# Output projection, second half: for each token tile the products with the first two head pairs first, for both column halves

## The chip, the cores and the metric

The kernel runs on one core of one Trainium2 chip. The metric is the device time of one execution, in microseconds (us). It is one launch that computes one transformer-like block on 512 tokens.

## The reference, cut to what matters

```python
z = h @ w_in                                    # h: adaLN-modulated RMSNorm of x, [512, 1024]
rec = _hgrn2(...)                               # 4 heads of 128: mix columns 0..511
att = _dsa_attention(...)                       # 8 heads of 64: mix columns 512..1023
mix = concatenate([rec, att]) @ w_out           # [512, 1024] @ [1024, 1024]
x = x + g1 * mix
h2 = _rms(x, norm2_g) * (1 + sc2) + sh2
x = x + g2 * _hier_moe(h2, ...)                 # router (4 + 16 logits), top group, top 2 of 4 experts;
                                                # 16 experts: (silu(h2 @ w1) * (h2 @ w3)) @ w2
```

All of it is float32. The vectors g1, sc2, sh2, g2 come from `silu(c) @ w_ada`, whose last parts are still being computed while attention ends.

## The kernel before, in words

**Precision by splitting.** A float32 product is made of three faster ones. A weight piece of 128 x 1024 (`raw`) is cast to `wh` on ACT, and DVE subtracts to get the rest `wl`. The activations are split the same way, into two halves of a tile `mix`. One call of `mm3` is three products of 128x512: mix-high by wh, mix-high by wl, mix-low by wh. `split_gen` does this for the pieces of w_in and then for the eight pieces of w_out, NZ to NZ+7, each after DVE has multiplied it by `g1b` (so that the projection comes out gated). Piece NZ + 4*half + 2*c + p holds the rows of two k-tiles (`mix` 4*half+2p and the next) and the columns of half c.

**Who sets the order.** Each step of the program is a Python generator. A small list scheduler, `Desk`, runs at build time: it takes the generator whose next step could start first by its own estimates (ties by a table of ranks), and so writes one fixed instruction order for each engine. Every engine then runs its list strictly in order and waits by semaphores. All instructions are recorded by one helper line, L177, so the program's tile names say what a row is. DMAs that carry their own line numbers (L1290, L1291) are issued by ACT from its own list.

**The output projection.** `out_gen` has two halves. Half 0 multiplies mix 0 to 3 (the recurrence's heads). Half 1 multiplies mix 4 to 7 (four pairs of attention heads, attention unit j gives mix 4+j) and runs while the last attention unit, attention 3, ends. Half 1 goes over four token tiles t and in each over the two column halves c. For one (t, c) a PSUM bank of the tag `z` (there are two such banks) collects 12 products: six with mix 4 and 5 (p = 0, piece NZ+4+2c) and six with mix 6 and 7 (p = 1, piece NZ+5+2c). `add_gen` then adds the bank to the residual `xm[t]` on DVE, and that frees the bank.

**What follows a tile.** `post_gen(t)` is started when tile t reaches c = 1. For each column half (kh) it transposes xm on PE (`a<-cs,xm`, four of 128x128, a PSUM tile `a`), copies the result to `hT` on ACT, and multiplies by the router's weights on PE (`u<-wr,hT` for even tiles, `o<-wr,hT` for odd ones, four for each kh). `norm_gen` squares and sums on ACT (`sc`). Then DVE makes the logits `L` and the second pass of `h2` (`h<-h,ss,sh2b`), `store_gen` lets ACT issue two DMAs (h2 and xm to memory, 512 KB each), and the routing follows on DVE. `first_gen` gathers the first expert's tokens when all tiles are through (`z<-oh,h`), and the MoE products (`h<-wh,xh`, ...) come after these.

**The end of attention 3.** PE makes `u<-PT,vv` (16 products, the attention's output), and then a chain follows whose parts are on different engines: `sq` on ACT, a mean by products on PE (`a<-sq,csm`), Ln and Exp on ACT, a multiplication on DVE, `mix` on ACT and DVE. Beside it, the last steps of adaLN run: `acc<-dd,cT,acc` on DVE, `a<-acc,ones` on PE, which lead to sh2b and gs2b and their transposes (`a<-cs,sh2b`, `a<-cs,gs2b`). One of the pieces, NZ+5, gets its place in a pool `mw` that can only be opened when attention 0 to 3 are done.

Of the kernel before, what the change touches and what calls it, by code (L numbers as in the profile page):

```python
# [9 lines left out]
F32 = mybir.dt.float32  # L10
F32R = mybir.dt.float32r
BF16 = mybir.dt.bfloat16
# [3 lines left out]
OP = mybir.AluOpType  # L16
# [4 lines left out]
T, D, P = 512, 1024, 128  # L21
# [3 lines left out]
MARK = -3e38  # L25
# [8 lines left out]
TMP2 = {"nl": 2, "oh": 3, "sq": 2, "zs": 2}  # L34
# [35 lines left out]
class Desk:  # L70
# [26 lines left out]
    def spawn(self, gen, name, rank):  # L97
        self.count += 1
        self.tasks.append(Task(gen, name, RANK[rank], self.at, self.last, self.count))

    def mark(self, name):
        self.done[name] = self.at
# [110 lines left out]
def hymba_kernel(ctx, tc, x, xT, w_ada1, w_ada, w_in, w_out, w_r, w1, w3, w2, vec, n2g, rb, rel, cst, t5, out):  # L213
    nc = tc.nc
    desk = Desk()
    spawn, mark, run = desk.spawn, desk.mark, desk.run
    sp = nc.sync
    act, dve, pool, pe = (desk.engine(e, n) for e, n in (
        (nc.scalar, "act"), (nc.vector, "dve"), (nc.gpsimd, "pool"), (nc.tensor, "pe")))
# [13 lines left out]
    def place4(tag, shape, dtype, name):  # L233
        return ar.tile(shape, dtype, tag=tag, name=name)
# [6 lines left out]
    def bank(shape=None, tag="a"):  # L241
        return ps.tile(shape or [P, 512], F32, tag=tag, name=tag, bufs=BANKS[tag])


    def slot_bank(shape=None, tag="a"):
        yield tag, BANKS[tag]
        return bank(shape, tag), desk.take(tag)
# [11 lines left out]
    def either(size):  # L259
        e = yield {"dve": size * EITHER_D, "pool": size * EITHER_P}  # L260
        return pool if e == "pool" else dve
# [16 lines left out]
    def C(n):  # L278
        a, b = CST[n]
        if b <= CST_W:  # L280
            return cs[:, a:b]
        off = CST["bo64"][0]
        return csm[:, a - off:b - off]
# [19 lines left out]
    area = [None]  # L303

    def tmp(tag, name, shape=None, dtype=F32):
        own, bufs = area[0]
        return own.tile(shape or [P, T], dtype, tag=tag, name=name, bufs=bufs[tag])
# [5 lines left out]
    pair = [None] * KT  # L313
# [21 lines left out]
    NZ = len(order)  # L335
    stream = [w_in[i] for i in order] + [w_out[i] for i in range(8)]
    raws, halves = {}, {}

    def fetch(n):
        if n < len(stream):  # L340
            raws[n] = ring()
            sp.dma_start(raws[n], stream[n])
            desk.done["raw", n] = desk.move()

    def split_gen():
        for n in range(len(stream)):

            need = ["mw"] if n == NZ + 5 else [("used", n - (WPB if HEAD + WPB <= n < NZ + 5 else HEAD if n < NZ else 4))]
            yield [("raw", n)] + (need if HEAD <= n < NZ else ["ada0"] * (n >= NZ))
            raw = raws.pop(n)  # L350
            if n >= NZ:
                eng = yield from either(1.0)
                rv = raw.rearrange("p (k c) -> p k c", k=2)
                c = (n - NZ) // 2 % 2
                eng.tensor_tensor(rv, rv, g1b[:, None, c * 512:c * 512 + 512].to_broadcast([P, 2, 512]), op=OP.mult)
                yield need
            yield "act"
            if WPB <= n < HEAD:
                wh, wl = (place4(f"B{2 * (n - WPB) + i}", [P, D], F32R, "wB") for i in range(2))
            else:  # L360
                own, bufs = (mw, WX) if n == NZ + 5 else (wp, WPB)
                wh = own.tile([P, D], F32R, tag="wh", name="wh", bufs=bufs)
                wl = own.tile([P, D], F32R, tag="wl", name="wl", bufs=bufs)
            act.copy(wh, raw)
            eng = yield from either(1.0)
            eng.tensor_tensor(wl, raw, wh.bitcast(F32), op=OP.subtract)
            halves[n] = wh, wl
            mark(("split", n))
            fetch(n + RING)
# [108 lines left out]
    def mm3(o, ah, al, bh, bl, start, stop):  # L478
        pe.matmul(o, ah, bh, start=start, stop=False)
        pe.matmul(o, ah, bl, start=False, stop=False)  # L480
        pe.matmul(o, al, bh, start=False, stop=stop)
# [33 lines left out]
    spawn(chunk_gen(), "chunks", "split")  # L515
    spawn(norm1_gen(), "norm1", "norm")
    spawn(split_gen(), "splits", "split")
    spawn(line_gen(), "line", "pz")
    for n in range(HEAD):
# [7 lines left out]
    gp = mixer.enter_context(ExitStack())  # L527
# [458 lines left out]
    def mod_rows(dst, r):  # L986
        pool.dma_start(dst, bass.AP(tensor=modD.tensor, offset=modD.offset + r * 512, ap=[[0, P], [1, D]]))
        return desk.move()
# [160 lines left out]
    def gate_gen():  # L1149
        yield ["ada1"]  # L1150
        desk.at += 2500
        desk.at = mod_rows(g2b, 6)

    h2s, routed, px = [None] * 4, {}, []

    def out_gen():
        nonlocal mw, sel, oh0, pair2
        for half in range(2):
            if half:
                yield [("att", j) for j in range(4)]  # L1160
                gp.close()
                mw = ctx.enter_context(tc.tile_pool(name="mw", bufs=1, reuse_waits="tile"))
                mark("mw")
                area[0] = mw, TMP2
                for n, w, v in (("g1", 8, -MARK), ("gm", 8, None), ("em", 16, None), ("e8", 8, None),
                                ("e2", 8, -MARK), ("er", 16, None)):
                    routed[n] = mw.tile([P, 4, w], F32, name=n)
                    if v:
                        pool.memset(routed[n], v)
                sel = mw.tile([P, 4, 16], BF16, name="sel")  # L1170
                oh0 = tmp("sq", "oh0", [P, 4, P])
                pair2 = mw.tile([P, 4, 16, 5], BF16, name="pair")
                pool.tensor_copy(pair2[:, :, :, 0], C("tok")[:, 0:1, None].to_broadcast([P, 4, 16]))
                pool.tensor_tensor(pair2[:, :, :, 1], C("tokT")[:, :, None].to_broadcast([P, 4, 16]),
                                   C("tok")[:, 0:1, None].to_broadcast([P, 4, 16]), op=OP.subtract)
            for a, b in ((a, b) for a in range(4) for b in range(2)):
                c, t = (b, a) if half else (a // 2, a % 2 * 2 + b)
                tt = slice(t * P, (t + 1) * P)
                n = NZ + half * 4 + c * 2
                if half and c:  # L1180
                    spawn(post_gen(t), ("post", t), "post")
                o, mz = yield from slot_bank(tag="z")
                for p in range(2):
                    yield [("split", n + p)]
                    wh, wl = halves[n + p]
                    for k in range(2):
                        kt = 4 * half + 2 * p + k
                        yield [("mix", kt)]
                        mx = pair[kt]
                        kc = slice(k * 512, k * 512 + 512)  # L1190
                        yield "pe"
                        mm3(o, mx[:, 0, tt], mx[:, 1, tt], wh[:, kc], wl[:, kc], p + k == 0, p + k == 2)
                    if t == 3:
                        mark(("used", n + p))
                spawn(add_gen(half, c, t, o, mz), ("add", half, c, t), "use")

    def add_gen(half, c, t, o, mz):
        cc = slice(c * 512, (c + 1) * 512)
        yield [("x", t)] + [("add", 0, c, t)] * half
        yield "dve"  # L1200
        dve.tensor_tensor(xm[t][:, cc], xm[t][:, cc], o, op=OP.add)
        mark(mz)

    sel = oh0 = pair2 = None

    def post_gen(t):
        yield [("add", 1, 0, t)] + [("post", t - 2)] * (t > 1)
# [85 lines left out]
    def first_gen():  # L1293
        yield ["out", ("store", 0), ("sel", 0), ("turned", 3)] + [("add", 1, 1, t) for t in range(4)]
        for _ in range(2):
            t, _m = yield from slot_bank([P, 4, P], "z")
            px.append(t)
            yield "pe"
            pe.matmul(px[-1], onesb, trib[:, 0:1, None].to_broadcast([P, 4, P]), start=True, stop=False)
        for t in range(4):  # L1300
            yield [("store", t), ("sel", t)] + [("pr", 3)] * (t > 0)
            for k in range(KT):
                yield "pe"
                pe.matmul(px[k // 4][:, k % 4], h2s[t][:, k * P:(k + 1) * P], oh0[:, t],
                          start=False, stop=t == 3 and k % 4 == 3)

    spawn(rows_gen(), "rows", "rows")
    spawn(gate_gen(), "gate", "rows")
    spawn(out_gen(), "out", "out")
    spawn(first_gen(), "first", "first")  # L1310

    def split2(n):
# [85 lines left out]
    gate, w = (mw.tile([P, 4, n], F32, name=m) for n, m in ((2, "gate"), (1, "wn")))  # L1398
# [303 lines left out]
```

## Time and profile before

| what | us |
|---|---|
| three runs | 728.30, 727.78, 728.07 (median 728.07) |
| the profiled execution | 727.48 |
| its span in the trace | 725.6 |
| PE busy in the span | 683.1 |
| DVE busy | 630.9 |
| ACT busy | 439.0 |

The span is the time from the first to the last instruction of the trace; the profiled execution's own time is 1.9 us more. "Busy" leaves out the instructions that only issue or branch. A row of the timeline gives the start, the duration, the engine, the line, the operation with its tiles (out <- in) and the count of equal instructions in a row; a bracket gives the idle time of the engine ahead of it and what ended it. Products are pipelined, so the duration of one (0.4 us) is longer than the distance from one to the next (0.23 us).

### The profile page before, as it was taken

How to read it: one execution, taken by the hardware profiler on the slowest of the kernel's cores; microseconds unless marked ns; L12 is line 12 of the kernel's file. 1: busy time of each engine (PE TensorE's matmuls, PEld its weight loads, DVE VectorE, ACT ScalarE, POOL GpSimd, SP SyncE). 2: the span in 40 equal slices, each digit the busy share in tenths (PEclk: the TensorE clock that was granted, in tenths of full speed). 3: DMA queues.
4: the chain of work that ended last, by engine and by line, in shares of the span. 5: the costliest groups of instructions: out<-in, count | busy, mean ns of one | idle time of the engine just before them, and what ended most of it. 6: DMA issues, size and time to landing. Idle time of an engine off the chain costs nothing.

```text
span 725.6 us, 10941 instructions
## 1 busy us (share of the span) xinstructions
PE 683.1 (94%) x3794; PEld 530.9 (73%) x3794; DVE 630.9 (87%) x1057; ACT 439.0 (61%) x670; POOL 202.4 (28%) x104
## 2 busy tenths in 40 slices
PE   3999999999999999999889979999999999999993
PEld 1666778877778776667568858888888888888872
DVE  4637889999999987978866889999999999999991
ACT  4326664545557466553343458888777777777770
POOL 0120010001321321122200030165655655556412
PEclk9999999999999999999989999999999999999997
DMA  9947532231120324685697889999999999999502
GB/s 363 406 154 224 190 111 88 89 115 59 56 90 30 117 88 164 225 308 181 188 362 305 315 318 406 390 376 347 365 363 367 354 350 358 364 361 349 187 11 33
DMA packets 57388, 172.84 MB, mean 238 GB/s; under 512 B 11954, under 2 KB 12530, under 8 KB 56304
## 3 DMA queue, kind: packets, MB, share of 16 engines
q1 hardware_dynamic: 45168, 150.54, 56.1%
q0 software_dynamic: 10720, 17.24, 8.5%
q10 hardware_dynamic: 1440, 4.31, 1.5%
q8 instruction: 32, 0.52, 0.3%
q14 instruction: 28, 0.23, 0.1%
HBM read 167.50 MB, written 15.24 MB: 252 GB/s over the span
## 4 chain that ended last, share of the span: by engine, by line
PE 50%; DMA 21%; DVE 14%; issue 10%; ACT 3%; SPq 0%; POOL 0%; POOLq 0%; DVEq 0%; ACTq 0%
PE z L177 30%; PE a L177 14%; DMA w<-in_w_dram 13%; DVE wl L177 8%; DMA out_dram<-yo,idx 6%; PE u L177 2%; PE h L177 2%; PE o L177 2%; DMA dd<-in_w_ada_dram 1%; DMA chunk<-in_w_ada_dram 1%; DVE yo L177 1%; DVE xl L177 1%; DVE oh L177 1%; ACT wh L177 1%; ACT sq L177 1%
## 5 line engine op out<-in xcount | busy, mean ns | idle before, releaser
L177 ACT CAST wh<-w 128x1024 fp32r<-128x1024 f32 x168 | 174.5, 1054 | 44.2 <-PE h L177 30.9
L177 DVE TENSOR_TENSOR wl<-w,wh 128x1024 fp32r<-128x1024 f32 x168 | 196.6, 1216 | 2.4 <-ACT wh L177 2.0
L177 PE MATMUL z<-hx,wh 128*128 128x512 f32 x496 | 163.1, 409 | 1.1 <-DVE hx L177 0.6
L1358 POOL DMA_INDIRECT out_dram<-yo,idx x16 | 123.7, 7730 | 120.8 <-DVE wl L177 64.1
L177 PEld LDWEIGHTS z<-hx,wh 128*128 128x128 f32 x496 | 88.8, 189 | 27.1 <-issue 8.7
L177 PE MATMUL h<-wl,xh 128*128 128x512 f32 x256 | 101.4, 396 | 0.0
L177 PE MATMUL h<-wh,xh 128*128 128x512 f32 x256 | 100.8, 394 | 0.0
L177 PE MATMUL h<-wh,xl 128*128 128x512 f32 x256 | 100.6, 393 | 0.0
L177 ACT CAST wh<-raw 128x1024 fp32r<-128x1024 f32 x64 | 67.1, 1052 | 55.3 <-PE z L177 48.0
L177 PE MATMUL z<-hx,wl 128*128 128x512 f32 x248 | 97.6, 394 | 0.0
L177 DVE TENSOR_TENSOR wl<-raw,wh 128x1024 fp32r<-128x1024 f32 x64 | 81.6, 1286 | 6.8 <-ACT wh L177 6.5
L177 PEld LDWEIGHTS h<-wl,xh 128*128 128x128 f32 x256 | 48.5, 189 | 12.9 <-DVE wl L177 3.0
L177 PEld LDWEIGHTS h<-wh,xh 128*128 128x128 f32 x256 | 48.5, 189 | 10.2
L177 PEld LDWEIGHTS h<-wh,xl 128*128 128x128 f32 x256 | 48.4, 189 | 10.1 <-DVE xl L177 0.3
L177 PE MATMUL y<-wh,hh 128*128 128x512 f32 x128 | 53.0, 414 | 2.0 <-DVE yo L177 2.0
L177 PEld LDWEIGHTS z<-hx,wl 128*128 128x128 f32 x248 | 46.8, 189 | 10.3
L177 PE MATMUL y<-wl,hh 128*128 128x512 f32 x128 | 50.6, 396 | 0.0
L177 PE MATMUL y<-wh,hl 128*128 128x512 f32 x128 | 50.6, 395 | 0.0
L177 PE MATMUL z<-wh,mix 128*128 128x512 f32 x128 | 48.3, 421 | 0.0
L177 DVE SCALAR_TENSOR_TENSOR acc<-dd,cT,acc 128x512 f32<-128x512 f32 x56 | 43.8, 782 | 3.6 <-DMA dd<-in_w_ada_dram 3.0
L177 POOL TENSOR_TENSOR dd<-b 128x512 f32<-128x512 f32 (+1 forms) x14 | 17.2, 1242 | 93.5 <-PE a L177 79.0
L1353 POOL DMA_INDIRECT xe<-h2D,idx x15 | 17.1, 1140 | 80.5 <-DVE idx L177 46.3
(290 smaller groups left out, 1145.2 us busy)
## 6 DMA issues: line engine op xcount, KB each, us to landing
w<-in_w_dram SPq DMA_DIRECT2D x164, 512.0 KB
raw<-in_w_in_dram SPq DMA_DIRECT2D x33, 512.0 KB
dd<-in_w_ada_dram SPq DMA_DIRECT2D x64, 256.0 KB
raw<-in_w_dram SPq DMA_DIRECT2D x24, 512.0 KB
chunk<-in_w_ada_dram SPq DMA_DIRECT2D x8, 1024.0 KB
raw<-in_w_out_dram SPq DMA_DIRECT2D x8, 512.0 KB
lineR<-lineD POOLq DMA_DIRECT2D x4, 640.0 KB, 17.6
xt<-in_xT_dram SPq DMA_DIRECT2D x4, 512.0 KB
```

The source lines that it names most:

```text
L177: r = f(*a, **k)
L1353: pool.indirect_dma_start(out=dst, out_offset=None, in_=h2D, in_offset=bass.IndirectOffsetOnAxis(ap=ix, axis=0), bounds_check=T - 1, oob_i ...
L1358: pool.indirect_dma_start(out=out, out_offset=bass.IndirectOffsetOnAxis(ap=ix, axis=0), in_=y, in_offset=None, bounds_check=T - 1, oob_is_ ...
```

## The change

The second half of `out_gen` now opens both z banks of a tile at once, and goes through (p, c) in the order p0 c0, p0 c1, p1 c0, p1 c1 instead of c0 p0, c0 p1, c1 p0, c1 p1. `post_gen(t)` is started when the loop reaches p1 c0. The pool `mw` is opened by a task of its own, `places_gen`, so that `out_gen` no longer waits there for attention 0 to 3. The pieces of w_out are split in the order NZ+4, NZ+6, NZ+5, NZ+7. The number of products is the same.

```diff
     def split_gen():
-        for n in range(len(stream)):
+        for n in [*range(NZ + 5), NZ + 6, NZ + 5, NZ + 7]:
...
+    def places_gen():
+        nonlocal mw, sel, oh0, pair2
+        yield [("att", j) for j in range(4)]
+        gp.close()
+        mw = ctx.enter_context(tc.tile_pool(name="mw", bufs=1, reuse_waits="tile"))
+        mark("mw")
...
+        for t in range(4):
+            banks = []
+            for p in range(2):
+                for c in range(2):
+                    if p == 0:
+                        banks.append((yield from slot_bank(tag="z")))
+                    elif c == 0:
+                        spawn(post_gen(t), ("post", t), "post")
+                    o, mz = banks[c]
+                    yield from piece_mm(o, 1, c, p, t)
+                    if p:
+                        spawn(add_gen(1, c, t, o, mz), ("add", 1, c, t), "use")
...
+    spawn(places_gen(), "places", "load")
```

`piece_mm` holds the six products of one piece, unchanged. The places where the order of an engine's list changes, by the two programs' lists:

On PE, just ahead of the last `u<-PT,vv` products of attention 3 (the rows with a + are the first z products of half 1, tile 0, with mix 4 and 5):

```order
 L177 MATMUL a<-cs,nl 128x128 x4
+L177 MATMUL z<-wh,mix 128x512
+L177 MATMUL z<-wl,mix 128x512
+L177 MATMUL z<-wh,mix 128x512 x2
+L177 MATMUL z<-wl,mix 128x512
+L177 MATMUL z<-wh,mix 128x512 x2
+L177 MATMUL z<-wl,mix 128x512
+L177 MATMUL z<-wh,mix 128x512 x2
+L177 MATMUL z<-wl,mix 128x512
+L177 MATMUL z<-wh,mix 128x512
 L177 MATMUL u<-PT,vv 64x128 x8
```

So 12 products, tile 0's p0 for both column halves, now stand ahead of the 16 u products (eight in each of two PSUM tiles); before, they stood behind the `a<-acc,ones` products.

On ACT, at the end of tile 0 (h_3613 and h_3624 are tile 0's h2 in the two programs; the `hT` copy and the `sc` behind the DMAs are tile 1's, kh = 0):

```order
 L177 ACTIVATE ss_3086<-hsq 128x1
 L177 ACTIVATE ss_3086<-ss_3086 128x1
-L1290 DMA h2D<-h_3613 128x1024
-L1291 DMA out_dram<-xm 128x1024
-L177 ACTIVATE sc,hsq<-xm 128x512
+L177 ACTIVATE sc,hsq<-xm 128x512
+L1305 DMA h2D<-h_3624 128x1024
+L1306 DMA out_dram<-xm 128x1024
 L177 COPY hT<-a 128x512
```

The two DMAs stand ahead of tile 1's first `hT` copy in both programs. On PE, between tile 0's last `u<-wr,hT` and tile 1's first `o<-wr,hT` stood 18 z products and four transposes; now there stand six z products and four transposes.

On PE and ACT, at tile 2 to tile 3. First PE before, the end of tile 3's c0 (z_3877 is the bank of c1, a_3889 the transposes, o_3888 the router's products):

```order
L177 MATMUL z_3877<-wh_3603,mix_2775 128x512
L177 MATMUL a_3889<-cs_75,xm_3074 128x128 x4
L177 MATMUL z_3877<-wh_3646,mix_3210 128x512
L177 MATMUL z_3877<-wl_3647,mix_3210 128x512
L177 MATMUL z_3877<-wh_3646,mix_3210 128x512
L177 MATMUL z_3877<-wh_3646,mix_3528 128x512
L177 MATMUL z_3877<-wl_3647,mix_3528 128x512
L177 MATMUL z_3877<-wh_3646,mix_3528 128x512
L177 MATMUL o_3888<-wr_3083,hT_3887 128x20 x4
```

Then PE in the changed program (a_3899 and o_3898 are the same steps):

```order
L177 MATMUL z_3848<-wh_3614,mix_3547 128x512
L177 MATMUL z_3848<-wl_3615,mix_3547 128x512
L177 MATMUL z_3848<-wh_3614,mix_3547 128x512
L177 MATMUL a_3899<-cs_75,xm_3074 128x128 x4
L177 MATMUL o_3898<-wr_3083,hT_3897 128x20 x4
```

And ACT in the changed program, the stores of tile 2 and what stands behind:

```order
L1305 DMA h2D_92<-h2_3817 128x1024
L1306 DMA out_0_dram<-xm_3073 128x1024
L177 CAST wh_3888<-w_3653 128x1024
L177 ACTIVATE sc_3900,hsq_3088<-xm_3074 128x512
L177 COPY hT_3897<-a_3899 128x512
```

The six z products that stood between the transposes and the router's products are now ahead of both, 12 z products stand between tile 2's last `u<-wr,hT` and a_3899, and ACT's list has a cast of a MoE weight between the stores and `hT`.

## Rows read from the trace of the kernel before

**Rows 1.** The page's first line.

```profile
span 725.6 us, 10941 instructions
```

**Rows 2.** Stretches: busy us of PE, PEld, DVE, ACT, POOL (instructions); granted clock; DMA share; GB/s.

```profile
365.00:368.30 3.30, 3.30 (x22) 2.44 (x23) 3.19 (x3) 0.27 (x1) 0.59 (x1) 0.50 1.00 392
368.30:378.60 10.30, 9.07 (x58) 7.45 (x56) 4.73 (x8) 5.28 (x9) 0.57 (x1) 1.00 1.02 402
378.60:404.20 25.60, 25.56 (x150) 21.44 (x149) 17.66 (x51) 10.51 (x26) 0.00 (x0) 1.00 0.72 274
440.00:690.00 250.00, 250.00 (x1220) 203.35 (x1219) 249.59 (x289) 198.97 (x222) 131.00 (x26) 1.00 0.96 351
```

**Rows 3.** PE in order, attention 3's last head pair and the pause: start, duration, [idle <-releaser].

```profile
355.21 0.43 PE L177 MATMUL u<-PT,vv 128*64 128x128 f32 x2
...
355.99 1.09 PE L177 MATMUL u<-PT,vv 128*64 128x128 f32 x14 [0.34 <-ACT PT L177]
...
364.94 0.68 PE L177 MATMUL a<-acc,ones 128*32 128x128 f32 x8 [4.99 <-DVE acc L177]
...
365.97 0.80 PE L177 MATMUL z<-wh,mix 128*128 128x512 f32 x1
...
368.54 0.60 PE L177 MATMUL a<-cs,sh2b 128*128 128x128 f32 x4
```

**Rows 4.** DVE around the copy of PT.

```profile
353.90 0.68 DVE L177 COPY PT<-a 128x512 f32<-128x512 f32 x1
354.51 0.68 DVE L177 TENSOR_TENSOR xm<-xm,z 128x512 f32<-128x512 f32 x1
```

**Rows 5.** DVE, products of pieces of w_out with g1: ns min/median/max.

```profile
L177 DVE TENSOR_TENSOR raw<-raw,g1b x7: 1211/1216/1718, 300.2 to 373.3; 128x1024 f32<-128x1024 f32 x7
```

**Rows 6.** ACT, the square root's input of attention 3.

```profile
357.11 0.60 ACT L177 ACTIVATE sq<-u 128x512 f32<-128x512 f32 x1 [1.18 <-PE u L177]
```

**Rows 7.** PE in order, tile 0's second column half before the change.

```profile
372.17 0.48 PE L177 MATMUL z<-wh,mix 128*128 128x512 f32 x1
...
373.20 0.50 PE L177 MATMUL z<-wl,mix 128*128 128x512 f32 x1 [0.56 <-DVE wl L177]
...
373.78 0.60 PE L177 MATMUL a<-cs,sh2b 128*128 128x128 f32 x4
...
374.13 0.48 PE L177 MATMUL z<-wh,mix 128*128 128x512 f32 x1
...
374.91 0.60 PE L177 MATMUL a<-cs,gs2b 128*128 128x128 f32 x4
...
377.31 0.50 PE L177 MATMUL z<-wl,mix 128*128 128x512 f32 x1 [0.67 <-DVE wl L177]
```

**Rows 8.** PE in order, tile 0 to tile 1.

```profile
382.18 0.48 PE L177 MATMUL z<-wh,mix 128*128 128x512 f32 x1
...
385.00 0.60 PE L177 MATMUL a<-cs,xm 128*128 128x128 f32 x4
...
385.35 0.47 PE L177 MATMUL z<-wh,mix 128*128 128x512 f32 x1
```

**Rows 9.** DVE, second pass of h2, tile 0.

```profile
382.86 1.28 DVE L177 SCALAR_TENSOR_TENSOR h<-h,ss,sh2b 128x1024 f32<-128x1024 f32 x1
```

**Rows 10.** ACT in order, stores of tile 0 and what follows; last a cast of a MoE weight.

```profile
384.17 0.34 ACTq L1290 DMA_DIRECT2D h2D<-h  x1
...
385.09 0.63 ACT L177 ACTIVATE sc<-xm 128x512 f32<-128x512 f32 x1 [3.89 <-DVE gm L177]
...
385.72 0.57 ACT L177 COPY hT<-a 128x512 f32<-128x512 f32 x1
...
403.38 1.05 ACT L177 CAST wh<-w 128x1024 fp32r<-128x1024 f32 x1
```

**Rows 11.** PE in order, first MoE product.

```profile
414.53 0.47 PE L177 MATMUL h<-wh,xh 128*128 128x512 f32 x1
```

**Rows 12.** Waits from 414 to 726 us: total, times, longest.

```profile
ACT wh L177 <- DMA w<-in_w_dram: 0.8, 2, 0.5
```

More of the change, by code (lines that the diff above doesn't have):

```diff
@@ L1152, in gate_gen @@
         desk.at = mod_rows(g2b, 6)
+    sel = oh0 = pair2 = None
     h2s, routed, px = [None] * 4, {}, []
-    def out_gen():
[L1157 to L1181, printed above, removed]
@@ new lines, in places_gen @@
+    def places_gen():
[4 more added lines that the diff above has]
+        mark("mw")
+        area[0] = mw, TMP2
+        for n, w, v in (("g1", 8, -MARK), ("gm", 8, None), ("em", 16, None), ("e8", 8, None),
+                        ("e2", 8, -MARK), ("er", 16, None)):
+            routed[n] = mw.tile([P, 4, w], F32, name=n)
+            if v:
+                pool.memset(routed[n], v)
+        sel = mw.tile([P, 4, 16], BF16, name="sel")
+        oh0 = tmp("sq", "oh0", [P, 4, P])
+        pair2 = mw.tile([P, 4, 16, 5], BF16, name="pair")
+        pool.tensor_copy(pair2[:, :, :, 0], C("tok")[:, 0:1, None].to_broadcast([P, 4, 16]))
+        pool.tensor_tensor(pair2[:, :, :, 1], C("tokT")[:, :, None].to_broadcast([P, 4, 16]),
+                           C("tok")[:, 0:1, None].to_broadcast([P, 4, 16]), op=OP.subtract)
@@ new lines, in piece_mm @@
+    def piece_mm(o, half, c, p, t):
+        tt = slice(t * P, (t + 1) * P)
+        n = NZ + half * 4 + c * 2 + p
+        yield [("split", n)]
+        wh, wl = halves[n]
+        for k in range(2):
+            kt = 4 * half + 2 * p + k
+            yield [("mix", kt)]
+            mx = pair[kt]
+            kc = slice(k * 512, k * 512 + 512)
+            yield "pe"
+            mm3(o, mx[:, 0, tt], mx[:, 1, tt], wh[:, kc], wl[:, kc], p + k == 0, p + k == 2)
+        if t == 3:
+            mark(("used", n))
@@ L1182, in out_gen @@
+    def out_gen():
+        for c in range(2):
+            for t in range(4):
                 o, mz = yield from slot_bank(tag="z")
                 for p in range(2):
[L1184 to L1192, printed above, removed]
@@ L1193, in out_gen @@
-                    if t == 3:
-                        mark(("used", n + p))
-                spawn(add_gen(half, c, t, o, mz), ("add", half, c, t), "use")
+                    yield from piece_mm(o, 0, c, p, t)
+                spawn(add_gen(0, c, t, o, mz), ("add", 0, c, t), "use")
+        for t in range(4):
+            banks = []
+            for p in range(2):
+                for c in range(2):
+                    if p == 0:
[6 more added lines that the diff above has]
+                        spawn(add_gen(1, c, t, o, mz), ("add", 1, c, t), "use")
@@ L1202, in add_gen @@
         mark(mz)
-    sel = oh0 = pair2 = None
     def post_gen(t):
```

## The prediction

> **What bounds the kernel now.** I read the first line of the page for the span [rows 1]: 725.6 us, while the profiled execution took 727.48, so 1.9 lie outside and stay as they are; the sum is made against 727.48, which is 0.6 below the median of the runs (728.07). Then I read the table by stretches [rows 2]. From 440 to 690 us PE is busy 250.00 of 250.00 and DVE 249.59: what the MoE does there doesn't depend on this change, and it ends as much later as it starts. Two checks that nothing catches the delay: in the waits behind 414 us the casts wait for weight loads for 0.8 us in all [rows 12], so the loads aren't the bound and wouldn't give back time; and the first MoE product follows the end of the projection directly, at 414.53 [rows 11]. So the change is worth what it does to the time 414.53, and that is PE's business: from 378.60 to 404.20 PE is busy 25.56 of 25.60, from 368.30 to 378.60 9.07 of 10.30. The only large hole is the one before 364.94, where PE idles 4.99 us until DVE's last `acc` [rows 3]. Behind the hole the granted clock is 0.50 until 368.3 (of the two levels, 1.2 GHz), and then 1.00 (2.4 GHz) [rows 2].
>
> To the eye the change then has an obvious gain: products with mix 4 and 5 need nothing of attention 3, so they could run in that hole. Whether they do is read from the lists.
>
> **The change part by part.**
>
> *The head.* The list of the changed program has the 12 products of tile 0's p0 not in the hole but ahead of the u products of attention 3. What do they cost there? Twelve such products take 382.18 to 385.00 = 2.82 [rows 8], 0.235 each. PE comes to them at 355.21 [rows 3] and to u at 355.21 + 2.82 = 358.03. In before u waits 0.34 for the copy of PT and runs its last 14 products from 355.99; now the copy has been made long before, even though DVE gets two instructions of a piece of w_out ahead of it: 353.90 + 1.22 (wl) + 0.68 (xm) + 1.22 (raw by g1, by its median) + 0.68 (the copy) = 357.70 at most [rows 4, 5], and with the longest raw, 1.72, 358.20. So the 14 start at 358.03 + 0.15 for two products (14 take 355.99 to 357.08, 0.075 each) = 358.18 instead of 355.99: **2.2 later**. Everything hangs on u: `sq` on ACT starts at 357.11 directly behind it [rows 6], the mean, Ln, Exp, the multiplication and `mix` follow one another, and DVE, in its list's order, can make the last `acc` only between them. PE's products on `acc` move from 364.94 to 367.1, and the 4.99 us hole stays as long as it was. Bounds: 2.2 if only that; 2.8 if also the new cast of wh on ACT ahead of the softmax's last step holds that up (half of its 1.05 [rows 10], since PE is not waiting there now); nothing cheaper, because PE runs in order.
>
> What goes away behind the hole: c0's six p0 products, which took 365.97 to 368.54 = 2.57 because the clock stood at half [rows 2, 3], and c1's six, 372.17 to 373.78 and 374.13 to 374.91 = 2.39, of which 0.56 is a wait for `wl` [rows 7]. Work gone: 2.57 + 1.83 = **4.4**. The two waits for `wl` (0.56 and 0.67, 1.23 together [rows 7]) are not lost but moved: the pieces NZ+5 and NZ+7 still become ready only late, the last of them by raw, cast and wl in a chain on DVE and ACT (1.22 + 1.05 + 1.22 [rows 5, 10]) that starts when DVE has come out of attention 3's chain. I take 0.9 for what PE waits, **0.3 less** (bounds: all of 1.23 as before, or none left). And the slow clock remains: after a hole of the same length it will be at 0.50 for some 2.3 us beyond the `acc` products (365.97 to 368.3), and now slows other products; products at half clock in 2.3 us lose 1.2, and where it falls into the waits it loses nothing. I take **+0.8** (bounds 0 and 1.2). Head: +2.2 − 4.4 − 0.3 + 0.8 = **−1.7** by the end of tile 0's products.
>
> *The tail: ACT's list.* PE from tile to tile is full now because between two router products that need `hT` there are 18 z products. Take U, the end of tile 0's last `u<-wr,hT`, 382.18 [rows 8]. DVE then makes the logits and the second pass of h2, 382.86 to 384.14 [rows 9]; ACT issues the two DMAs, which wait for that, from 384.17, and its next instruction starts at 385.09 [rows 10], U + 2.91. In both programs tile 1's first `hT` copy is behind these two DMAs. Before, `sc` comes first and `hT` ends at 385.72 + 0.57 = 386.29, U + 4.11, when PE is still in the 18 products (18 × 0.235 + 0.35 for four transposes, 385.00 to 385.35 [rows 8], = U + 4.58). Now `sc` is done ahead of the DMAs, so `hT` ends at U + 2.91 + 0.57 = U + 3.48, but PE has only six products and four transposes, 6 × 0.235 + 0.35 = U + 1.76. PE stands **1.7**. The next tile has it worse: between tile 2's last router product and tile 3's first, PE has 12 products and the transposes, 2.82 + 0.35 = U + 3.17; ACT has the DMAs (U + 2.91), a cast of 1.05 [rows 10], `sc` (0.63 from its start to `hT`) and `hT` 0.57: U + 5.16. PE stands **2.0**. Tile 1 to tile 2 has 21 z products and the transposes, U + 5.3, against `hT` at U + 4.1 (DMAs, `sc`, `hT`): no stall. The sum of the stalls is 3.7; since ACT may come a little earlier where DVE's second pass doesn't have the 0.68 of an addition ahead of it, I take **3.6** (bounds: 0 if DVE's second pass came early enough in both, 4.5 if a store waited for an earlier one to land). The Trainium skill (DMA: Bandwidth & Descriptors, "Issuing engines are not separate DMA queues") says that the issuing engine's time to initiate a DMA is usually small relative to the DMA. Here it is 385.09 − 384.17 = 0.92 us for two, and the row decides; taken as nothing, both stalls would be 0.92 shorter and the total near no change, which is part of rival B.
>
> *The other edits.* Opening `mw` in its own task and splitting NZ+6 before NZ+5 add no instruction; what they move is counted above. Nothing is added to DMA queues but order. Number of products equal: z work in the tiles 1 to 3 is the same.
>
> Total: −1.7 + 3.6 = **+1.9**: 727.48 becomes 729.4, and the median 728.07 becomes 730.0.
>
> **Rivals.**
>
> *B, the stores don't stand in the way (faster).* If the second pass of h2 comes early enough, because DVE has less ahead of it than in before, ACT issues before PE needs `hT`. For: DVE is busy only 17.66 of 25.60 us in that stretch [rows 2]. Against: the logits need PE's last router product, U itself, and the second pass stands behind the logits on DVE; U + 1.96 for its end is the same in every tile. It decides at `hT` before U + 1.76 (tile 1) and U + 3.17 (tile 3). If both stalls are gone, the head's −1.7 stays: 726.4; if one only, or if the issue of the DMAs costs nothing and both shrink by 0.92, 728.0 to 728.4.
>
> *C, the head gives nothing.* The change then doesn't do what it says: the 12 products are moved, but the chain's delay with 2.8, all of 1.2 for the clock and waits of 1.9 (0.7 more than before, for pieces that come later with the chain) give 2.8 − 4.4 + 0.7 + 1.2 = +0.3. With the stalls: +3.9, 732.0. For: the hole in PE is not filled. Against: 4.4 us of work really leave the stretch behind it.
>
> *D, the banks don't come free.* Both z banks now fill within a tile, and the first must be emptied by DVE while only the second's last six products run: cover 6 × 0.235 = 1.4 instead of 2.82. Emptying takes about 0.4 (a product's length) + 0.68 [rows 4], 1.1 in all; where DVE is in a second pass of h2 (1.28 [rows 9]) it takes 2.4 and PE waits 1.0. At four of the turnovers: about +3.6 on top, 733.6. Against: transposes and router products fill some of the same time. The Trainium skill (Perfetto Trace Analysis, "Matmuls") asks that independent groups rotate through banks so that evacuation overlaps the next group's products: by that rule this order is the worse one.
>
> **How the numbers follow.** The forecast (both stalls come, head −1.7, give or take 1) has 0.58, B 0.25 (0.12 with both stalls gone, 0.13 with one), C 0.09, D 0.08. Such a measurement can tell about 0.2%, 1.5 us, from no change. Of the forecast's 0.58, 0.15 lie below 1.5 us: faster 0.12, same 0.15 + 0.13 = 0.28, slower 0.43 + 0.09 + 0.08 = 0.60. The range leaves out B with both gone (0.12) and D (0.08): 727.4 to 732.0. The forecast's own range, by the bounds of the head's terms, is 729 to 731.
>
> **What would show it.** In the profile of the changed kernel: 12 z products ahead of u, `sq` at about 359.3, a PE hole of about 5 us that ends at about 367.1 with `acc`; a PE stall of about 1.7 ahead of tile 1's first `o<-wr,hT` and of about 2.0 ahead of tile 3's, both released by ACT's `hT`; the first MoE product at about 416.4. Wrong would be: a hole much shorter than 4.99 (then the moved products did fill it), no wait for `hT`, or waits of z products for DVE's xm.

## The result

The changed kernel takes 732.63 us in the median of 17 executions (729.01 to 736.23), the kernel before 727.78 (727.05 to 729.98): the ratio is 1.0063, with an interval of 1.0051 to 1.0075. It is slower, as forecast, but by some 4.6 us (by the ratio; the two medians lie 4.85 apart) where 1.9 were forecast, and 0.6 above the upper end of the range. What stands out beside the median is the spread: 7.2 us, where the kernel before has 2.9 here (and 5.0 to 5.6 in the larger groups that were run beside the experiments).

The first line of the page of the changed kernel (its profiled execution took 733.37):

```profile
span 731.5 us, 10944 instructions
```

The timeline of PE, of the changed kernel, from attention 3's output to the first MoE product (columns as ahead of the prediction: start, duration, operation, count, idle time and what ended it):

```profile
357.87 1.09 PE L177 MATMUL u<-PT,vv 128*64 128x128 f32 x16
...
366.84 0.68 PE L177 MATMUL a<-acc,ones 128*32 128x128 f32 x8 [5.00 <-DVE acc L177]
...
387.50 1.31 PE L177 MATMUL o<-wr,hT 128*128 128x20 f32 x8 [1.45 <-ACT hT L177]
...
389.39 0.78 PE L177 MATMUL z<-wh,mix 128*128 128x512 f32 x1
...
406.84 1.07 PE L177 MATMUL o<-wr,hT 128*128 128x20 f32 x8 [1.82 <-ACT hT L177]
...
411.55 5.24 PE L177 MATMUL z<-oh,h 128*128 128x128 f32 x28
...
420.49 0.47 PE L177 MATMUL h<-wh,xh 128*128 128x512 f32 x1
```

Each step of the prediction can be found. u starts at 357.87, with no wait ahead of it [rows 3: 355.99 for its last 14]. The hole behind ends at 366.84 and is 5.00 us long [rows 3: 4.99]. Two stalls are new, 1.45 and 1.82, both ended by ACT's `hT`, at tile 1's and tile 3's first router products. ACT's timeline shows why:

```profile
386.00 0.34 ACTq L1305 DMA_DIRECT2D h2D<-h  x1
...
386.38 0.45 ACTq L1306 DMA_DIRECT2D out_dram<-xm  x1
...
386.86 0.58 ACT L177 COPY hT<-a 128x512 f32<-128x512 f32 x1 [2.70 <-DVE hsq L177]
...
403.52 0.33 ACTq L1305 DMA_DIRECT2D h2D<-h  x1
...
403.89 0.67 ACTq L1306 DMA_DIRECT2D out_dram<-xm  x1
...
404.65 1.05 ACT L177 CAST wh<-w 128x1024 fp32r<-128x1024 f32 x1 [3.75 <-DVE em L177]
...
406.23 0.56 ACT L177 COPY hT<-a 128x512 f32<-128x512 f32 x1
```

At 386.00 and 403.52 ACT issues the stores, and the copies `hT` (386.86 and 406.23) stand behind them, the second one behind a cast as well. From the first store to the next instruction are 0.86 us, in the kernel before 0.92 [rows 10]. So far it is the forecast: 1.45 + 1.82 = 3.27 where 3.6 was said.

What no step said of these stalls is in the granted clock. The table by stretches for PE (stretch, length, busy us and instructions, granted clock, DMA share, GB/s):

```profile
386.00:388.00 2.00, 0.55 (x6) 1.00 1.03 420
...
388.60:391.30 2.70, 2.70 (x10) 0.50 1.03 419
...
402.00:406.00 4.00, 3.02 (x16) 1.00 0.96 333
...
410.00:412.00 2.00, 2.00 (x11) 0.50 1.03 420
...
417.00:418.00 1.00, 1.00 (x11) 1.00 0.56 217
```

Behind each of the two stalls the clock is at 0.50, of the two levels the lower. The 28 products `z<-oh,h` from 411.55 take 5.24 us. In the kernel before the same row reads:

```profile
407.27 3.37 PE L177 MATMUL z<-oh,h 128*128 128x128 f32 x28
```

The first MoE product stands at 420.49 [rows 11: 414.53], 5.96 later, and the span is 731.5 − 725.6 = 5.9 longer. So in this pair of traces the whole loss lies in this stage, and the MoE hands it on unchanged, as said.

Since executions differ in what lies ahead of this stage, I measure the stage from the last `a<-cs,nl` products (354.69 in the kernel before, 354.59 in the changed one) to the first MoE product: 59.84 before, 65.90 after.

### The profile page after: what moved, and what is told of

The parts are those of the page before. It is cut to its first block, busy times and chain, and to the rows that moved or that the text cites. A ratio compares the mean times of both kernels' runs of the same rounds, so it can differ in the third digit from the quotient of the medians.

```text
span 731.5 us, 10944 instructions
## 1 busy us (share of the span) xinstructions
PE 686.9 (94%) x3794; PEld 535.6 (73%) x3794; DVE 631.3 (86%) x1057; ACT 438.8 (60%) x670; POOL 201.8 (28%) x104
## 4 chain that ended last, share of the span: by engine, by line
PE 49%; DMA 21%; DVE 15%; issue 9%; ACT 3%; SPq 0%; POOL 0%; ACTq 0%; POOLq 0%; DVEq 0%
PE z L177 29%; PE a L177 14%; DMA w<-in_w_dram 9%; DVE wl L177 8%; DMA out_dram<-yo,idx 8%; PE o L177 2%; PE u L177 2%; PE h L177 2%; DMA dd<-in_w_ada_dram 2%; DMA raw<-in_w_dram 1%; DMA chunk<-in_w_ada_dram 1%; DVE xl L177 1%; DVE oh L177 1%; ACT sq L177 1%; ACT wh L177 1%
```

## The experiments

Every time below is a median of 6 to 12 executions (17 for the result). The kernel before was run beside each group on the same chip: 728.23 (726.64 to 731.68) with the first stores on GpSimd, the first filler, p0 in the hole, and p0 in the hole with GpSimd's stores; 729.01 (727.05 to 732.32) with the change again, the stores behind hT, the second filler and tiles 1 to 3 only; 727.93 (726.58 to 732.17) with the other four. "Before" and "the change" in the table are the pair of the result.

| kernel | us (lowest to highest) | ratio to before, interval | stage in the trace | waits for hT in it |
|---|---|---|---|---|
| before | 727.78 (727.05 to 729.98) | | 59.84 | none |
| the change | 732.63 (729.01 to 736.23) | 1.0063, 1.0051 to 1.0075 | 65.90 | 1.45, 1.82 |
| the change again | 732.24 (729.34 to 736.64) | 1.0046, 1.0013 to 1.0079 | 61.43 | 1.44, 0.16, 1.72 |
| stores on GpSimd | 725.49 (723.39 to 729.17) | 0.9964, 0.9948 to 0.9980 | 58.26 | 0.68 |
| stores behind hT | 727.14 (724.78 to 729.66) | 0.9967, 0.9940 to 0.9994 | 58.87 | 0.67 |
| filler | 731.25 (729.54 to 734.05) | 1.0051, 1.0031 to 1.0072 | 61.06 | none over 0.3 |
| filler again | 729.89 (728.16 to 734.69) | 1.0013, 0.9982 to 1.0044 | 61.54 | 0.34 |
| tiles 1 to 3 only | 733.29 (730.93 to 735.24) | 1.0050, 1.0023 to 1.0076 | 65.41 | 1.76 |
| stall by copies | 734.72 (730.86 to 739.99) | 1.0090, 1.0061 to 1.0120 | 66.55 | 1.14, 2.53 |
| p0 in the hole | 731.20 (729.03 to 736.48) | 1.0053, 1.0029 to 1.0077 | 65.72 | 1.45, 0.38, 1.86 |
| hole, stores on GpSimd | 724.61 (723.05 to 729.45) | 0.9956, 0.9937 to 0.9976 | 58.94 | 0.67 |
| before, stores on GpSimd | 726.25 (725.09 to 729.78) | 0.9970, 0.9951 to 0.9988 | 60.64 | none |
| hole, DVE's list, stores behind hT | 727.45 (724.86 to 731.20) | 0.9986, 0.9965 to 1.0007 | (list differs) | 0.87, 0.68 |
| hole, DVE's list, stores on GpSimd | 725.49 (723.01 to 727.33) | 0.9952, 0.9934 to 0.9971 | (list differs) | 0.68 |

**The changed kernel again.** No edit; a second trace.

> The changed kernel itself, for a second trace and a median beside the others on one chip. Theory: the same waits of 1.45 and 1.82 for hT, and 0.50 behind at least one of them; how long it lasts differs between executions, which is the spread of 7 us. Rival, the waits differ between executions and the clock doesn't.

The second trace, of an execution of 729.34 us, is the control that the first lacked. PE's timeline:

```profile
387.94 1.07 PE L177 MATMUL o<-wr,hT 128*128 128x20 f32 x8 [1.44 <-ACT hT L177]
...
406.08 1.07 PE L177 MATMUL o<-wr,hT 128*128 128x20 f32 x8 [1.72 <-ACT hT L177]
...
409.39 3.37 PE L177 MATMUL z<-oh,h 128*128 128x128 f32 x28
```

And its clock behind the two stalls:

```profile
388.00:396.00 8.00, 8.00 (x50) 1.00 0.99 403
...
408.00:415.00 7.00, 6.98 (x65) 1.00 1.01 378
```

The same waits, 1.44 and 1.72, but 1.00 behind both, and the 28 products take 3.37. The stage is 61.43 long, 1.59 more than before; with the clock at 0.50 it was 65.90, 4.5 us more. From the first stall's end to the second's are 18.14 us here and 19.34 in the first trace, and from there to the first MoE product 10.57 and 13.65. So, with the small differences of the waits taken out, 4.3 of the 4.5 us stand behind the two stalls and are what the low clock cost in the first execution; it cost nothing in the second, while the stalls were alike (3.27 and 3.32). One half of the theory on record holds: the waits stay, and what differs between executions is the clock. The other half doesn't: 0.50 behind at least one of the waits was expected, and here it is behind neither.

Two traces are few, but the mean granted clock of the whole span is on record for every execution. Of the 17 of the result the four fastest (729.01 to 730.92 us) have 0.985 to 0.987; of the five slowest (735.11 to 736.23) four have 0.975 or 0.976 and one 0.981. The traced ones fit in: 733.37 us with 0.980, 729.34 with 0.987. So the spread of the change goes with the clock, and the median execution (732.63 us, 0.982) lies nearer the first trace than the second.

**Stores on GpSimd.**

```diff
-        act.dma_start(h2D[t * P:(t + 1) * P, :], h2)
-        act.dma_start(out[t * P:(t + 1) * P, :], xm[t])
+        pool.dma_start(h2D[t * P:(t + 1) * P, :], h2)
+        pool.dma_start(out[t * P:(t + 1) * P, :], xm[t])
```

> The changed kernel with the two stores of each tile (h2 and xm) issued by GpSimd in place of ACT; PE's and DVE's lists stay the same, ACT's loses only the eight DMAs. Theory: the waits for hT (1.45 and 1.82 us) come from ACT's list, where the stores stand ahead of hT, and the low clock behind them (0.50) comes from these waits; so both go, the first MoE product starts near 412.8, and the time is 728 - 1.7 = 726.3. Rival 1, the low clock has nothing to do with the waits: the waits go, the stretches at 0.50 behind 388 and 408 stay, about 730. Rival 2, DVE's second pass of h2 or the z banks hold PE: the waits stay, 732.6.

725.49, where 726.3 was expected, and the stage is 58.26. PE's one wait for `hT`, at tile 3, and the clock around it:

```profile
404.96 1.07 PE L177 MATMUL o<-wr,hT 128*128 128x20 f32 x8 [0.68 <-ACT hT L177]
...
385.00:415.00 30.00, 29.31 (x208) 1.00 0.94 363
```

One wait of 0.68 is left where 1.82 was, none at tile 1, and the granted clock is 1.00 from 385 to 415. Rival 1 falls, since the low clock went with the waits; so does rival 2, since neither DVE's second pass nor the banks hold PE. But the time is lower than the stage explains, by 2.0 us: from the start of the last scatter to the end of the program were 9.6 us before and 7.6 now. So a second kernel keeps the queue and changes only the place.

**Stores behind hT.**

```diff
             act.copy(hT[:, kh * 4:kh * 4 + 4], pt)
+            mark(("ht", t, kh))
...
+        if t < 3:
+            yield [("ht", t + 1, 0)]
         act.dma_start(h2D[t * P:(t + 1) * P, :], h2)
```

> The changed kernel with the stores still on ACT, but each tile's pair behind the next tile's first hT copy in ACT's list instead of ahead of it; the lists of PE and DVE stay the same. Theory: it is the place in ACT's list, not the queue; both waits for hT (1.45 and 1.82) fall under 0.7, the clock stays at 1.00 behind them, and the first MoE product follows the last a<-cs,nl by about 60.0 - 1.7 + 0.5 = 58.5 to 59 us (59.7 in the kernel before, 65.9 in the changed one). The run with GpSimd's stores also ended 2.0 us sooner behind the last scatter; here that should not show: about 727.3. Rival, GpSimd's queue itself brought the gain: waits as in the changed kernel, 732.6.

ACT's timeline of this kernel, tile 0 to tile 1, with the copy now ahead of the stores:

```profile
385.47 0.59 ACT L177 COPY hT<-a 128x512 f32<-128x512 f32 x1 [0.53 <-PE a L177]
...
386.77 0.34 ACTq L1308 DMA_DIRECT2D h2D<-h  x1
...
387.15 0.45 ACTq L1309 DMA_DIRECT2D out_dram<-xm  x1
```

And PE's only wait for `hT`, and the first MoE product:

```profile
403.60 1.07 PE L177 MATMUL o<-wr,hT 128*128 128x20 f32 x8 [0.67 <-ACT hT L177]
...
414.21 0.47 PE L177 MATMUL h<-wh,xh 128*128 128x512 f32 x1
```

Its clock, from behind the old hole to the MoE:

```profile
372.00:426.00 54.00, 49.08 (x321) 1.00 0.93 354
```

Nothing else moved in the lists of PE and DVE, and the time falls from 732.24 to 727.14 on the same chip, to just under the kernel before (0.9967). The place in ACT's list was the cause of the stalls, not the queue. The stage is 58.87, in the range expected (58.5 to 59) and 0.97 less than before; with the 0.67 that is still waited, the change's head is worth −1.64 by this trace.

**Filler.** Seven extra products whose result is overwritten; the output stays the same. (The router's PSUM tile is made a whole bank for them, in lines not shown.)

```diff
...
             yield "pe"
+            if kh == 0 and t % 2:
+                for _ in range(7):
+                    nc.tensor.matmul(po, onesb, trib[:, 0:1].to_broadcast([P, 512]), start=True, stop=True)
             for k in range(4 * kh, 4 * kh + 4):
```

> The changed kernel with seven extra products of two constant bf16 tiles (onesb by trib, 128x512, into the router's bank, overwritten at once) on PE right ahead of the first router products of tiles 1 and 3, where PE waits for hT; nothing else moves. It adds work and takes no wait away. Theory: PE no longer stands idle there, so the granted clock stays at 1.00 behind, and the time falls by what the low clock cost (4.4 us in the profiled run): 728 - 1.7 + 3.3 = 729.6, with a smaller spread between runs than the 7 us of the changed kernel. Rival 1, the low clock has nothing to do with the idle PE: 732.6 as before or up to 3 more, and the same spread.

> The filler run once more, beside the changed kernel on the same chip, since six runs spread over 4.5 us. Theory: the trace again shows 1.00 from 385 to 420; its median lies under the changed kernel's, by up to 4.4. Rival, the low clock is as frequent with the gap filled: no difference of the medians.

PE's timeline of the first filler run: the extra products stand where PE was idle, and the router products come with no wait to speak of.

```profile
385.89 1.47 PE L1249 MATMUL o<-trib,onesb 128*128 128x512 bf16 x6
...
387.27 1.07 PE L177 MATMUL o<-wr,hT 128*128 128x20 f32 x8
...
403.33 1.47 PE L1249 MATMUL o<-trib,onesb 128*128 128x512 bf16 x6
...
404.84 1.07 PE L177 MATMUL o<-wr,hT 128*128 128x20 f32 x8
```

The table by stretches of the same run, from tile 1's filler on:

```profile
388.00:396.00 8.00, 8.00 (x49) 1.00 0.89 284
...
406.00:416.00 10.00, 9.98 (x91) 1.00 0.97 385
```

The clock is at 1.00 throughout. The stage is 61.06 and 61.54 in the two traces, with more work on PE, and the stores where they were. That is as long as in the second trace of the change (61.43), where PE was idle and the clock did not fall, and 4.4 to 4.8 shorter than in the first. The medians say less than the traces: the first time 731.25, where 729.6 was expected; the second 729.89 against 732.24 on one chip, six executions each, with intervals that overlap. And the spread did not shrink (4.5 and 6.5 us). Both traces are of fast executions (the fastest and the third of their six), and so is the trace of the change that shows 1.00 without a filler. So the clock stayed up in both filler traces, but that the filler keeps it up is not shown.

A part of the spread isn't from these two gaps at all: the kernel before, which doesn't have them, spreads over 5.0 and 5.3 us in the same two groups. Its older waits have stretches at 0.50 behind them that differ from trace to trace. Behind the 5 us hole the stretch lasts 3.4 us in the kernel before and 6.0 in the second filler trace. Behind PE's 3.2 us wait for DVE's `oh` in the MoE's first expert, which all these kernels have, 0.50 lasts from 426.4 to 429.7 in the kernel before and from 426.0 to 432.7 in the first filler trace, and in the trace of the kernel before with GpSimd's stores the clock stays at 1.00 there.

**Stall by copies.** The converse: the kernel with the stores behind hT, held up at the same places with no store in the way.

```diff
+            if kh == 0 and t % 2:
+                for _ in range(3):
+                    nc.scalar.copy(hT[:, 0:4], pt)
             act.copy(hT[:, kh * 4:kh * 4 + 4], pt)
```

> The kernel with the stores behind hT, and in it ACT makes the first hT copy of tiles 1 and 3 four times over, which holds PE up at the same two places as in the changed kernel, by about 1.2 and 2.3 us, without a DMA in the way. Theory: it is PE's idle time that costs, whatever makes it: 727.1 + 3.3 = 730.4 for the waits alone, and in a part of the executions the clock at 0.50 behind them and up to 5 more, so a median of 731 to 733. Rival, the low clock belongs to the DMAs issued there: 730.4 with a spread no larger than that of the kernel with the stores behind hT.

PE's timeline at its two waits for `hT`:

```profile
390.37 1.07 PE L177 MATMUL o<-wr,hT 128*128 128x20 f32 x8 [1.14 <-ACT hT L177]
...
410.87 1.07 PE L177 MATMUL o<-wr,hT 128*128 128x20 f32 x8 [2.53 <-ACT hT L177]
```

And the stretches behind them:

```profile
392.00:394.00 2.00, 2.00 (x6) 0.50 1.03 416
...
413.00:417.00 4.00, 4.00 (x19) 0.50 0.97 334
```

The waits are 1.14 and 2.53, and 0.50 stands behind both. The stage is 66.55, against 58.87 without the copies: 7.7 us for 3.0 us of additional waiting (1.14 + 2.53 − 0.67). So the waits are enough; no store has to stand in front of the copy. The median, 734.72, came above the 731 to 733 expected. The mean granted clock of the ten executions, 0.971 to 0.987, against 0.983 to 0.988 without the copies, says that the low clock is behind that; how often it fell behind each wait is not known.

**Tiles 1 to 3 only.** The head of the change is taken out: tile 0, the order of the pieces and the opening of `mw` are as before.

```diff
-        for n in [*range(NZ + 5), NZ + 6, NZ + 5, NZ + 7]:
+        for n in range(len(stream)):
...
+            steps = [(0, 0), (0, 1), (1, 0), (1, 1)]
+            if t == 0:
+                steps = [(0, 0), (1, 0), (0, 1), (1, 1)]
...
```

> The kernel before with the new order in tiles 1 to 3 alone; tile 0, the order of the weight pieces and the opening of mw stay as they were. The head of the change is gone, and tile 0 to tile 1 keeps its cover; tile 3's router products stand directly behind the transposes, as in the changed kernel. Theory: one wait for hT of about 1.9 and the low clock behind it: 728.2 + 1.9 and 0 to 3.3 for the clock = 730.1 to 733.4. Rival, the head (12 products ahead of u) is what makes the kernel slow: 728.2, no change.

PE's timeline at its one wait for `hT`:

```profile
407.02 1.07 PE L177 MATMUL o<-wr,hT 128*128 128x20 f32 x8 [1.76 <-ACT hT L177]
```

The clock ahead of it and behind:

```profile
400.00:405.00 5.00, 5.00 (x29) 1.00 0.68 232
...
410.00:414.00 4.00, 4.00 (x21) 0.50 0.99 374
```

As slow as the whole change without its head: 733.29 (730.1 to 733.4 expected), against 732.24 on the same chip. The stage is 65.41, 5.6 longer than before. From the wait's end to the first MoE product are 13.63 us, against 10.57 with the clock up, so the wait of 1.76 and the 3.1 us behind it make up most of that; some 1.2 lie ahead of it, where the stretch at 0.50 behind the old hole lasted 5.9 us instead of 3.4. So the tail's order alone makes the kernel slow.

**p0 in the hole.**

```diff
         pe.matmul(ms, C("sel2")[0:2], d2, start=False, stop=True)
+        mark(("ms", j))
...
+        yield [("ms", 3)]
         for t in range(4):
             banks = []
```

> The changed kernel with tile 0's 12 p0 products behind attention 3's a<-sq,csm and a<-d,csm products instead of ahead of u, that is in PE's hole of 5.0 us. Theory: u is 1.9 to 2.2 us earlier again, the hole shrinks to about 2.2, the waits for hT and the low clock behind them stay: 732.6 - 2.1 = 730.5, and up to 1.2 less if the clock doesn't fall in the shorter hole. Rival, the products delay the chain in the new place as well: no change, 732.6.

PE's timeline, u and the end of the hole:

```profile
358.13 1.58 PE L177 MATMUL u<-PT,vv 128*64 128x128 f32 x16 [2.23 <-DVE PT L177]
...
368.49 0.45 PE L177 MATMUL a<-acc,ones 128*32 128x128 f32 x8 [2.06 <-DVE acc L177]
```

DVE's timeline ahead of the copy of PT and with it:

```profile
354.52 1.22 DVE L177 TENSOR_TENSOR wl<-raw,wh 128x1024 fp32r<-128x1024 f32 x1
...
356.25 1.22 DVE L177 TENSOR_TENSOR raw<-raw,g1b 128x1024 f32<-128x1024 f32 x1
...
357.39 0.68 DVE L177 COPY PT<-a 128x512 f32<-128x512 f32 x1
```

The clock behind u's wait, and behind the last wait for `hT`:

```profile
358.60:362.00 3.40, 3.40 (x30) 0.50 0.59 177
...
410.00:416.00 6.00, 6.00 (x30) 0.50 1.00 384
```

The hole did shrink from 5.00 to 2.06. But u waits 2.23 for DVE's copy of PT, which stands behind `wl` and `raw` in DVE's list, and starts only 0.45 earlier (2.83 behind the last `a<-cs,nl`, against 3.28 in the change). Behind this new wait the clock is at 0.50 as well: u's 16 products take 1.58 instead of 1.09, so that they end no earlier, and the products on `acc` start 13.19 behind the last `a<-cs,nl`, against 12.24 in the two traces of the change. The median, 731.20, is near the 730.5 expected, but the stage (65.72, with 0.50 behind the 1.86 alone of its waits for `hT`) gained nothing, so the theory on u falls: the 12 products and DVE's two instructions each hold u for about 2.2 us, side by side, and taking away one leaves the other. Together with the stores on GpSimd:

> Both edits: tile 0's p0 products in the hole, and the stores issued by GpSimd. Theory: head -1.7 - 2.1, no waits for hT, no low clock behind 385: 728 - 3.8 = 724.2, down to 723 if the clock doesn't fall in the shorter hole. Rival 1 (low clock untied to the waits): about 728. Rival 2 (DVE or banks hold PE): about 730.

724.61, near the 724.2 expected, but 2.2 of its gain are the end of the program; its stage, 58.94, is no shorter than with the stores alone (58.26).

**Both holders of u taken away.** The one edit that is new; the other two are shown above.

```diff
-            yield [("raw", n)] + (need if HEAD <= n < NZ else ["ada0"] * (n >= NZ))
+            yield [("raw", n)] + (need if HEAD <= n < NZ else ["ada0"] * (n >= NZ)) + [("unit", 3, 3, 0)] * (n in (NZ + 5, NZ + 6))
```

> The changed kernel with three edits: tile 0's p0 products in PE's hole, the pieces NZ+5 and NZ+6 split only after DVE's copy of PT, and the stores behind hT. Theory: u is no longer held by the 12 products nor by DVE's list, so it comes 2.2 us earlier than in the kernel with the stores behind hT: 727.1 - 2.2 = 724.9, and up to 1.5 less if the shorter hole leaves the clock up. Rival, the chain behind u is bound by something else (the acc products on DVE): 727.1.

> The same with the stores issued by GpSimd in place of behind hT. Theory: another 2.0 at the end of the program: 722.9 (724.6 in the run without the change to DVE's list, less 2.2: 722.4). Rival as for the other: 724.6.

Neither gained what was expected (724.9 and 722.9): 727.45 and 725.49, near their rivals (727.1 and 724.6). PE's timeline of the first shows where it went:

```profile
354.45 1.09 PE L177 MATMUL u<-PT,vv 128*64 128x128 f32 x16
...
363.38 0.50 PE L177 MATMUL z<-wh,mix 128*128 128x512 f32 x1 [0.86 <-ACT wh L177]
...
366.77 0.79 PE L177 MATMUL z<-wl,mix 128*128 128x512 f32 x1 [2.88 <-DVE wl L177]
```

u comes 1.92 behind the last `a<-cs,nl`, where the change has 3.28, and the hole before `acc` is gone; but the pieces that were split later are now themselves late, and PE waits 0.86 and 2.88 for their wh and wl. The scheduler also moved other products of half 0 there, so these two are no clean test of the head; they show that the wait moved.

**The kernel before with the stores on GpSimd.**

> The kernel before with the stores issued by GpSimd; PE's list stays. In its trace PE never waits for hT, so by the theory the stage of the projection takes the same time (first MoE product 59.8 behind the last a<-cs,nl); only the end of the program, 2.0 sooner behind the last scatter in the two runs with GpSimd's stores, can give something: 726. Rival, the stores on ACT cost the stage something in the kernel before as well: under 725.

726.25 with the stage no shorter (60.64, 0.80 longer than in the kernel before, whose PE list it shares; the stretch at 0.50 behind the hole lasts 5.5 us here and 3.4 there). From the last scatter's start to the end of the span: 725.0 − 717.59 = 7.4, in the kernel before 725.6 − 716.02 = 9.6. The last scatter in GpSimd's timeline, with the stores there:

```profile
717.59 1.55 POOL L1358 DMA_INDIRECT out_dram<-yo,idx  x1 [5.37 <-DVE yo L177]
```

And in the kernel before:

```profile
716.02 1.54 POOL L1358 DMA_INDIRECT out_dram<-yo,idx  x1 [5.27 <-DMA out_dram<-yo,idx]
```

The four traces with GpSimd's stores have 7.4 to 7.6 there, the ten with ACT's 9.4 to 9.7. So these 2 us belong to the engine that issues the stores and have nothing to do with the change.

## Why the prediction was wrong

**The head: right in its sum, partly by luck.** "Head: −1.7" was the sum of four terms. The second trace gives 61.43 − 59.84 − 3.32 = −1.73, the kernel with the stores behind hT −1.64, the one with GpSimd's stores −2.26. One trace tells this to about 0.8 us, the difference of the stage in two traces of the old PE list (59.84 and 60.64). The 5 us hole stayed as long (5.00), and its end moved by 2.0 (2.2 forecast). The waits for `wl` fell from 1.23 to 0.57, which is −0.7 where −0.3 was forecast; with 4.4 for the work that went, +1.3 is left for the slow clock and all else, where +0.8 was forecast. So two terms missed in opposite directions, and that the sum fits to 0.1 is luck. The reason for the delay of u was half told: I priced the 12 products ahead of u and took DVE's copy of PT to be in time (357.70 against 358.03 worked out; 356.68 + 0.68 = 357.36 measured). It is in time only because PE is late; take PE's products away, and DVE holds u by the same amount.

**The stalls: right.** 1.7 and 2.0 were forecast, 3.6 together; 1.45 and 1.82 came, and 1.44, 0.16 and 1.72 the second time (the 0.16 at tile 2, where none was forecast). Both end with ACT's `hT`, and moving the stores in ACT's list takes them away.

**The step that failed: "PE stands 1.7 ... 2.0", priced at the idle time alone.** I had the clock in the sum, as +0.8 for the old hole, but gave the two new stalls none, although [rows 2] show 0.50 behind the one large idle stretch of the stage. The runs show what stood in its place. Behind the two stalls of the first trace the low clock cost 4.3 us, more than the stalls' own 3.3. Behind waits for `hT` of 1.1 us and more, the clock was at 0.50 in six of nine cases over five traces (the change twice, p0 in the hole, tiles 1 to 3 only, stall by copies), and in none of the seven waits of 0.34 to 0.87 in the others. With it the sum is −1.7 + 3.3 = +1.6 where the clock stays up, which is the 729.34 us execution, and +5.9 where it falls behind both, which is the 733.37 us one. The median lies between, nearer the second, at 4.6. So it was no rival that took the place of the forecast, but a term that its sum left out, and that came in some executions and not in others.

The Trainium skill has a case that belongs beside that row (TensorE: Matmul & The Clock Gate, "HAM oscillation — how this bites in real kernels"): a kernel in which PE waits for a DMA again and again, and the products behind each wait start at the lower clock, so that a wait costs more than its length. Its waits are longer than those here, and its rule is for such longer gaps, so that by it alone no low clock would be expected here. The measurement differs, and decides: six of nine waits of 1.14 to 2.53 us have 0.50 behind them, and the second trace of the change, with two equal waits and no low clock, shows that it isn't certain from one execution to the next.

**The rivals.** B, that the stores don't stand in the way, is out: they did. C, that the head gives nothing, is out. D, the banks, never showed: no z product waited for DVE's `xm` in the traces of the change. Slower, which had 0.60, came. The upper end of the range, built from C, was too low because no case had the clock behind the stalls in it.

What stays open: what decides in one execution whether the clock falls behind a wait of 1.4 to 1.9 us, and whether a filler changes that. Five of the medians are from 6 executions, with intervals of the ratio of up to ±0.33%, or 2.4 us; so smaller differences between experiments rest on the traces, one for each kernel, and not on the medians.

## What to carry to other kernels

When an order change takes products away between two waits of PE on another engine, price the new stall twice: once for its length and once for the work that runs behind it at the lower clock, here 4.3 us behind 3.3 us of stalls in one execution and nothing in another; and give the range both cases. Look at what stands in the in-order list of the engine that releases the wait: here two DMA issues ahead of each of two copies cost the change all its gain, and putting them behind the copies made the same change no slower than the kernel before. Where two engines hold an instruction by the same amount, taking one away shows nothing.

## What the runs showed that was not expected

The end of the program is 2.0 to 2.2 us shorter when ACT issues no stores in the middle: 7.4 to 7.6 us from the last scatter's start to the end, against 9.6 in the kernel before. This makes the kernel before 0.9970 of itself with no other edit. The lowest ratios here (0.9952 and 0.9956, both with p0 in the hole and the stores on GpSimd) contain the same 2 us, and can't be told apart by their intervals. Why the end takes less was not tried.

One and the same program has the clock at 0.50 behind both its waits of 1.4 to 1.8 us in one execution, and at 1.00 behind both in another.
